# A two-layer hybrid encoder in one kernel: a fixed issue order around the early gates, and the second layer's modulation computed in the first layer

## The chip, the cores and the metric

The kernel runs on one core of a Trainium2 chip. The metric is the device time of one execution in microseconds, and the time before is the median of three runs. TensorE multiplies, VectorE, ScalarE and GpSimd work element by element, SyncE (SP) only issues DMAs; ScalarE issues some DMAs too. Each engine takes its own instructions in a fixed order, and engines wait for one another through semaphores.

## The reference

The input is x (1024 tokens, 1024 channels, f32) and a vector c. Each of two layers does:

```
mod = silu(c) @ w_mod[l] + b_mod[l]           # sh1, sc1, g1, sh2, sc2, g2: six parts of 1024
h = rms_norm(x) * (1 + sc1) + sh1
y = mixer(h) @ w_out[l]                       # four head groups A, B, C, D over w_in[l]
x = x + g1 * rms_norm(y)
h = rms_norm(x) * (1 + sc2) + sh2
u = dwconv3(h @ w_up[l])                      # 2 x 2816 channels, 3 taps along the tokens
y = (gelu(u_gate) * u_value) @ w_down[l]
x = x + g2 * rms_norm(y)
```

The mixer is windowed attention (A), a short gated convolution (B), latent attention (C) and dilated windowed attention in three patterns (D).

## The kernel before

Channels lie on the partitions, tokens on the free axis; x and y are eight tiles of 128 x 1024. f32 operands are split into a high and a low fp32r half (`split`, L110 and L111: ScalarE copies the high half, GpSimd or VectorE subtracts for the low one), and a product is three matmuls, high x high, high x low and low x high.

A tile framework orders the work. The program is traced in Python; each engine's order is fixed ahead of the run by a list scheduler that, with a cost model, takes the ready instruction that was traced first. A helper `issue_after(ins)` adds an edge: every instruction traced in its block on the engine of `ins` is queued behind `ins`. Waits on data are added by the framework. Buffers are named by pool and tag, and a new tile of a tag waits until the older one in its place is free.

One layer goes through these stages:

- `mixer` (layer 0 up to 765 us, layer 1 from about 1700 to 2380). `group_d` computes values, keys and queries of the three patterns of D; between them it traces the modulation vectors of its own layer (`modulations`, parts 2, 4 and 3). One modulation part is 16 pieces: a 256 KB load of w_mod on SP and one VectorE instruction that accumulates (L360, L362), then a fold (L416 to L439).
- `project_out`, in two halves of 512 tokens. After each half comes `token_half`: `residual` (root of the mean square by `rstd`: squares on ScalarE at L164, column totals on TensorE at L158 with some added up on VectorE or GpSimd at L171, the root on VectorE from L176; then the scaling and x, L513 and L514), and `dense_input`, which does a second `rstd`, scales (L471), shifts (L474) and splits into `hh`, `hl`. For the second half `dense_input` goes through four pairs of tiles and also builds the sums that a Strassen-like product needs: t1 to t4, split into halves like the rest.
- `dense_up`: 22 pairs of a gate tile and a value tile, each by seven products of quarters (12 matmuls each) in place of eight. For the first six pairs (`ahead`) the two quarters that need only the first half's tokens run early, as `begin`: 12 matmuls into a bank `pj`, a copy to the tile u (L1238), 12 more into the same bank, a second copy (L1242), then the tile is stored to `kept`. Their weights (`early`) are loaded ahead of the second `token_half`, but the products are traced behind it. Then the weight sums of each pair (`sums`: two 512 KB loads, L1257 to L1262 on VectorE, three splits), the products of the first two pairs tile by tile (L1333), the four others of `ahead` (`kept_pair`), the rest, and after each pair `gated`: the convolution (first tap L934 on ScalarE for the gate of the first eight pairs, L936 on VectorE for all others; L938), GELU, the product (L1308) and a store.
- `dense_down`: blocks of two to four rows of tiles (`whole`, eight output tiles each; L1409 copies, L1411 adds to y), the rest in token halves (`some`, L1418), then the end of the layer. Layer 0 also does three modulation parts here ((0,5), (1,1) and (1,0)): `advance(2)` traces two pieces behind each output tile's addition, through two buffers `mr`. What is left over is traced before the end of the layer, which needs the room of these buffers.

`early`, `begin` and `sums` take their weight tiles in turn from three pairs of one pool and two of another (`pair`).

Of the kernel before, what the change touches and what calls it, by code (L numbers as in the profile page):

```python
# [9 lines left out]
F32 = mybir.dt.float32  # L10
F32R = mybir.dt.float32r
# [8 lines left out]
D = 1024  # L20
# [72 lines left out]
class Trunk:  # L93
# [51 lines left out]

    def rstd(self, tiles, n, temp, adders=None):

# [314 lines left out]

    def dense_input(self, y, l, half, temp, adders):

        nc, hs = self.nc, HALVES[half]
        rs = self.rstd([t[:, hs] for t in y], D, temp, adders)

        def normal(k):  # L470
            nc.vector.scalar_tensor_tensor(y[k][:, hs], y[k][:, hs], self.col(l, 2, k), rs, op0=ALU.mult, op1=ALU.mult)  # L471

        def shifted(k):
            nc.scalar.activation(y[k][:, hs], y[k][:, hs], AF.Identity, bias=self.shift(l, 3, k))  # L474

        if half == 0:
            for k in (0, 4, 1, 5, 2, 6, 3, 7):
                normal(k)
                shifted(k)
                self.split(self.hh[k][:, hs], self.hl[k][:, hs], y[k][:, hs], nc.gpsimd if k % 2 else nc.vector)  # L480
            return
        n1, n2 = HALVES
        self.t2, self.t3, self.t4w = [], [], []
        for i in range(4):
            j = 4 + i
            a, b, t12 = y[i], y[j], temp("x")
            t1, t2, t3, t4 = t12[:, n1], t12[:, n2], temp("sq"), temp("t")
            normal(i)
            normal(j)
            shifted(j)  # L490
            nc.vector.scalar_tensor_tensor(t1, a[:, n2], self.shift(l, 3, i), a[:, n1], op0=ALU.add, op1=ALU.subtract)
            nc.vector.tensor_sub(t2, b[:, n2], t1)
            nc.vector.tensor_sub(t4, b[:, n1], t2)
            nc.vector.tensor_sub(t3, t2, a[:, n1])
            self.split(self.hh[i][:, n2], self.hl[i][:, n2], t1, nc.vector)
            self.split(self.hh[j][:, n2], self.hl[j][:, n2], b[:, n2], nc.gpsimd if i % 2 else nc.vector)
            for to, k, t, eng in ((self.t2, i, t2, None), (self.t4w, None, t4, nc.vector), (self.t3, j, t3, None)):
                room = self.te.tile([128, 1024], F32R, name="t4", tag=f"t4{i}") if k is None else self.new_y(k, F32R)
                self.split(room[:, n1], room[:, n2], t, eng)
                to.append((room[:, n1], room[:, n2]))  # L500

# [595 lines left out]
    def mixer(self, l):  # L1097
        tc, nc = self.tc, self.nc
        with ExitStack() as e:
# [4 lines left out]
            with ExitStack() as e2:  # L1104
# [90 lines left out]
    def quarter(self, ps, w, at, xs, first=True, last=True, order=None):  # L1195
# [6 lines left out]
        for i, (xh, _) in enumerate(xs):  # L1202
            ks = slice(at + 128 * i, at + 128 * i + 128)
            nc.tensor.matmul(ps, w[1][:, ks], xh, start=False, stop=last and i == len(xs) - 1, skip_group_check=True)  # L1204

    def dense_up(self, l, early):
# [5 lines left out]
        n1, n2 = HALVES  # L1212
        b11 = [(self.hh[i][:, n1], self.hl[i][:, n1]) for i in range(4)]
        b21 = [(self.hh[i][:, n1], self.hl[i][:, n1]) for i in range(4, 8)]
# [3 lines left out]
        c1, c2 = slice(1, 513), slice(513, 1025)  # L1218
        ahead = 6
        kept = self.kept  # L1220
        with tc.tile_pool(name=f"ux{l}", bufs=2, reuse_waits="tile") as ux, \
# [4 lines left out]
            def u_tile():  # L1226
# [5 lines left out]
                return u  # L1232

            def begin(u, w1, between=None):

                x = self.pj.tile([128, 512], F32, name="pj", tag="pj")
                self.quarter(x, w1, 0, b11)
                nc.scalar.activation(u[:, c2], x, AF.Copy)  # L1238
                if between:
                    between()  # L1240
                self.quarter(x, w1, 512, b21, False)
                nc.scalar.activation(u[:, c1], x, AF.Copy)  # L1242

            def sums(t, whole):

                gate, sums = self.pair(F32)
                nc.sync.dma_start(gate, self.a["w_up"][l, t])
                raw = self.raw.tile([128, 1024], F32, name="raw", tag="raw")
                nc.sync.dma_start(raw, self.a["w_up"][l, FT + t])
                a11, a12, a21, a22 = (r[:, h] for r in (gate, raw) for h in HALVES)  # L1250
                w1 = self.pair() if whole else None
                w2, w3 = self.pair(), self.pair()
                if whole:
                    self.split(*w1, gate)
                w4 = [a2p.tile([128, 512], F32R, name=t, tag=t) for t in ("vh", "vl")]
                s1, s2 = sums[:, 0:512], sums[:, 512:1024]
                nc.vector.tensor_add(s1, a21, a22)  # L1257
                nc.vector.tensor_sub(s2, s1, a11)
                self.split(*w4, a22)

                nc.vector.tensor_sub(a21, a11, a21)
                nc.vector.tensor_sub(a22, a12, s2)  # L1262
                self.split(*w2, sums)
                self.split(*w3, raw)
                return w1, w2, w3, w4

# [35 lines left out]
            def gated(t, us):  # L1302
                cv = [self.tmp(x) for x in "ab"]
                for o, u, m in zip(cv, us, (t, FT + t)):
                    base = _P["fconv"] + l * 132 + m
                    self.conv3(o, u, lambda i: self.par[:, base + 44 * i:base + 44 * i + 1], m == t < ahead + 2)
# [5 lines left out]
            for t in range(ahead):  # L1312
                u = u_tile()
                begin(u, early[t] if t < len(early) else self.up_weight(l, t))
                nc.scalar.dma_start(kept[128 * t:128 * t + 128, :], u[:, 1:1025])

            def kept_pair(t):
                ws, u = sums(t, False), u_tile()
                nc.sync.dma_start(u[:, 1:1025], kept[128 * t:128 * t + 128, :])
                return Pair(u, ws)  # L1320


            two = [kept_pair(t) for t in range(2)]
            jobs = []
# [15 lines left out]
            for t in range(2, FT):  # L1340
                if t < ahead:
                    p = kept_pair(t)
                    p.head()
                else:
                    ws, u = sums(t, True), u_tile()
                    p = Pair(u, ws)
                    begin(u, ws[0], p.head)
                gated(t, p.tail())

    def dense_down(self, l, y, end):  # L1350
# [3 lines left out]
        with tc.tile_pool(name=f"dq{l}", bufs=4, reuse_waits="tile") as dq:  # L1354
# [96 lines left out]
    def run(self):  # L1451
# [13 lines left out]
        self.vd = [dram.tile([S, 260], F32, name=f"vd{p}") for p in range(2)]  # L1465
        self.brep = [dram.tile([4, 128, n], F32, name=f"brep{i}") for i, n in enumerate(OH_LEN)]
        self.setup()
        xsrc = a["x"]
# [30 lines left out]
        for l in range(DEPTH):  # L1499
# [108 lines left out]
```

## Time and profile before

| what | value |
|---|---|
| median of 3 runs | 3244.16 us (3235.51 to 3247.09) |
| profiled execution | 3242.23 us, span 3240.4 us |
| TensorE (PE) busy | 2884.5 us, 89%, 13178 matmuls |
| VectorE (DVE) busy | 2385.1 us, 74% |
| ScalarE (ACT) busy | 1159.5 us, 36% |
| GpSimd (POOL) busy | 1157.2 us, 36% |
| mean granted TensorE clock | 0.952 of full speed |
| DMA | 305.32 MB, 94 GB/s over the span |

All times inside the run count from the start of the span. A matmul of 128 x 128 by 128 x 512 is listed with about 0.4 us since matmuls overlap in the pipeline; how closely they follow each other is seen from their count in a stretch. "x6" behind a line is the number of merged instructions, and the brackets behind it give the idle time of the engine before the first of them and what ended it.

### The profile page before, as it was taken

The numbers are of one execution on the slowest core, as the hardware profiler recorded it, in microseconds if no ns is written. First come the engines' busy times: TensorE is split into PE (matmuls) and PEld (weight loads), VectorE is DVE, ScalarE is ACT, GpSimd is POOL, SyncE is SP. The second block draws the span as 40 slices with busy tenths as digits, with TensorE's granted clock in tenths as the row PEclk, the third lists the DMA queues.
The fourth block names the chain that finished last, engine by engine and source line by source line (L and its number), as shares of the span: only waits on it lengthen the run. The fifth ranks groups of instructions, "written<-read, shape, count | busy, mean of one in ns | idle before, by whom it ended". The sixth has DMA issues, their size and how long they took to land. (4 is left out here: it accounts for less than half of the span.)

```text
span 3240.4 us, 35414 instructions
## 1 busy us (share of the span) xinstructions
PE 2884.5 (89%) x13178; PEld 2291.8 (71%) x13178; DVE 2385.1 (74%) x3196; ACT 1159.5 (36%) x1674; POOL 1157.2 (36%) x821
## 2 busy tenths in 40 slices
PE   7888989988959999999979889898887789999997
PEld 3677767776637778878756777677765668887886
DVE  6687567697558888867767875577965798886556
ACT  4231443554433333331243223435534433234121
POOL 1221133324344554542532212232244545455231
PEclk8998999999979999999989999999998999999999
DMA  5225111102333222254422341110123232224323
GB/s 201 80 91 183 55 37 34 56 20 78 104 110 110 84 80 78 85 195 162 156 94 62 120 149 50 40 47 27 46 73 129 101 114 85 85 78 141 133 91 104
DMA packets 122680, 305.32 MB, mean 94 GB/s; under 512 B 13403, under 2 KB 32091, under 8 KB 122508
## 3 DMA queue, kind: packets, MB, share of 16 engines
q1 hardware_dynamic: 113868, 284.19, 26.6%
q10 hardware_dynamic: 8640, 18.88, 1.5%
q8 instruction: 103, 1.69, 0.2%
q14 instruction: 69, 0.57, 0.1%
HBM read 244.38 MB, written 62.03 MB: 95 GB/s over the span
## 5 line engine op out<-in xcount | busy, mean ns | idle before, releaser
L111 POOL TENSOR_TENSOR wl<-raw,wh 128x1024 fp32r<-128x1024 f32 (+2 forms) x82 | 203.8, 2486 | 468.4 <-ACT wh L110 259.0
L530 PE MATMUL pj<-hh,wh 128*128 128x512 f32 x800 | 331.1, 414 | 25.5 <-DVE ks L561 14.7
L531 PE MATMUL pj<-hl,wh 128*128 128x512 f32 x800 | 325.7, 407 | 6.4 <-POOL hl L459 5.3
L534 PE MATMUL pj<-hh,wl 128*128 128x512 f32 x800 | 210.7, 402 | 0.0
L530 PEld LDWEIGHTS pj<-hh,wh 128*128 128x128 f32 x800 | 156.6, 196 | 68.2 <-issue 30.6
L531 PEld LDWEIGHTS pj<-hl,wh 128*128 128x128 f32 x800 | 156.2, 195 | 44.1 <-POOL hl L459 7.3
L534 PEld LDWEIGHTS pj<-hh,wl 128*128 128x128 f32 x800 | 153.5, 193 | 36.3 <-issue 1.0
L690 PE MATMUL po<-s,v 128*96 128x128 f32 (+3 forms) x672 | 133.4, 360 | 43.8 <-ACT s L687 43.7
L690 PE MATMUL po<-hp,v 128*96 128x256 f32 x512 | 126.4, 402 | 36.3 <-ACT hp L687 35.9
L690 PEld LDWEIGHTS po<-s,v 128*96 128x96 f32 x672 | 99.3, 187 | 72.7 <-ACT s L687 56.2
L111 POOL TENSOR_TENSOR ul<-raw,uh 128x1024 fp32r<-128x1024 f32 x45 | 120.6, 2680 | 70.2 <-ACT uh L110 70.1
L577 ACT ACTIVATE qh<-pj 64x512 fp32r<-64x512 f32 x128 | 107.2, 837 | 99.4 <-PE pj L534 51.5
L110 ACT ACTIVATE wh<-raw 128x1024 fp32r<-128x1024 f32 (+2 forms) x90 | 94.0, 1044 | 134.4 <-PE pj L531 76.9
L938 DVE SCALAR_TENSOR_TENSOR ta<-u,par,ta 128x1024 f32<-128x1024 f32 x88 | 138.9, 1578 | 1.4 <-ACT ta L934 1.4
L1411 DVE TENSOR_TENSOR y<-y,po 128x1024 f32<-128x1024 f32 x60 | 73.0, 1218 | 90.4 <-PE po L523 90.4
L690 PEld LDWEIGHTS po<-hp,v 128*96 128x96 f32 x512 | 85.8, 172 | 71.4 <-ACT hp L687 44.0
L579 DVE TENSOR_TENSOR ql<-pj,qh 64x512 fp32r<-64x512 f32 x64 | 55.5, 867 | 107.3 <-ACT qh L577 106.5
L938 DVE SCALAR_TENSOR_TENSOR tb<-u,par,tb 128x1024 f32<-128x1024 f32 x88 | 128.2, 1457 | 0.0
L111 POOL TENSOR_TENSOR pl<-raw,ph 128x1024 fp32r<-128x1024 f32 x26 | 66.2, 2551 | 168.2 <-ACT ph L110 108.0
L677 PE MATMUL psc<-qh,ks 128*128 128x256 f32 (+2 forms) x272 | 88.3, 339 | 38.9 <-DVE s L805 15.2
L560 ACT ACTIVATE ks<-pj 64x512 fp32r<-64x512 f32 x56 | 49.0, 876 | 163.8 <-PE pj L534 96.5
L561 DVE TENSOR_TENSOR ks<-pj,ks 64x512 fp32r<-64x512 f32 x56 | 51.0, 911 | 73.6 <-ACT ks L560 72.8
(613 smaller groups left out, 8988.2 us busy)
## 6 DMA issues: line engine op xcount, KB each, us to landing
raw<-in_w_up_dram SPq DMA_DIRECT2D x56, 512.0 KB, 3.6
raw<-in_w_in_dram SPq DMA_DIRECT2D x52, 512.0 KB, 3.3
raw<-in_w_down_dram SPq DMA_DIRECT2D x50, 512.0 KB, 3.7
mr<-in_w_mod_dram SPq DMA_DIRECT2D x96, 256.0 KB, 3.0
room<-in_w_mod_dram SPq DMA_DIRECT2D x96, 256.0 KB, 3.4
actd<-ta SPq DMA_DIRECT2D x44, 512.0 KB, 2.6
uh<-in_w_up_dram SPq DMA_DIRECT2D x26, 512.0 KB, 3.7
xd<-y ACTq DMA_DIRECT2D x48, 256.0 KB, 3.6
```

The source lines that it names most:

```text
L110: self.nc.scalar.activation(hi, src, AF.Copy)
L111: (eng or self.nc.gpsimd).tensor_sub(lo, src, hi.bitcast(F32))
L530: nc.tensor.matmul(ps, wh[:, ks], self.hh[k][:, hs], start=k == 0, stop=False, skip_group_check=True)
L531: nc.tensor.matmul(ps, wh[:, ks], self.hl[k][:, hs], start=False, stop=False, skip_group_check=True)
L534: nc.tensor.matmul(ps, wl[:, ks], self.hh[k][:, hs], start=False, stop=k == KT - 1, skip_group_check=True)
L561: nc.vector.tensor_sub(lo, src, hi.bitcast(F32))
L577: nc.scalar.activation(self.perm(qh[h][o:o + 64], r)[:, n * half:n * half + n, :], src, AF.Copy)
L579: nc.vector.tensor_sub(lo, src, own.bitcast(F32))
L677: nc.tensor.matmul(ps, ks[:, c], qh[:, q0:q1], start=first, stop=False, skip_group_check=True)
L690: nc.tensor.matmul(o[0:96, co], v(tt, h), s[:, cs], start=co.start // 512 not in seen, stop=False, skip_group_check=True)
L938: nc.vector.scalar_tensor_tensor(o, t[:, i:i + n], cw(i), o, op0=ALU.mult, op1=ALU.add)
L1411: self.mark = nc.vector.tensor_add(d, d, p)
```

## The change

- In the second half's `token_half` the order of tracing becomes: residual, the six early gates (`begin_early`), the weight sums of the first two pairs, and only then `dense_input`. The early gates alternate between two tiles of u (they had four) and skip the memsets of the edge columns; the first two pairs' w4 halves lie in tiles `ta` and `tb`.
- Edges in `dense_input` of the second half: the first four squares behind gate 1's second copy, the last four behind gate 2's (both on ScalarE), the totals behind gate 3's last matmul (on TensorE), and what ScalarE does for the four pairs of tiles behind the second copies of gates 4, 5, 5 and 5.
- The modulation parts 2, 4 and 3 of layer 1 leave the second mixer. The list of pieces in layer 0 has six parts in place of three; the up-projection of layer 0 traces one piece after each of the pairs 6 to 21, and the large blocks of `dense_down` three behind each output tile in place of two.
- The first tap of the convolution is on ScalarE for the gate of all 22 pairs.

```diff
 rstd:
-            nc.scalar.activation(sq, t, AF.Square)
+            with self.queued(after and after[0][i]):
+                nc.scalar.activation(sq, t, AF.Square)
             if eng is nc.tensor:
-                total(sq, first, i == len(tiles) - 1 and not accs)
+                with self.queued(after and after[1]):
+                    total(sq, first, i == len(tiles) - 1 and not accs)
 dense_input:
+        rs = self.rstd([t[:, hs] for t in y], D, temp, adders,
+                       after and ([after[1][1]] * 4 + [after[2][1]] * 4, after[3][0]))
...
         for i in range(4):
+            with self.queued(after[min(4 + i, len(after) - 1)][1]):
...
+    def queued(self, ins):
+        return self.tc.issue_after(ins.ins) if ins is not None else ExitStack()
 mixer:
-                self.group_d(l, self.modulations(l))
+                self.group_d(l, self.modulations(l) if l == 0 else iter(()))
+    def begin_early(self, l, ws):
+        nc, done = self.nc, []
+        for t in range(self.ahead):
+            u = self.t4.tile([128, 1026], F32, name="u", tag=("tc", "tn")[t % 2])
+            done.append(self.begin(u, ws[t] if t < len(ws) else self.up_weight(l, t)))
+            nc.scalar.dma_start(self.kept[128 * t:128 * t + 128, :], u[:, 1:1025])
+        return done
 dense_up:
-                    self.conv3(o, u, ..., m == t < ahead + 2)
+                    self.conv3(o, u, ..., m == t)
-            two = [kept_pair(t) for t in range(2)]
+            two = [kept_pair(t, ws) for t, ws in enumerate(early)]
...
                 gated(t, p.tail())
+                if t >= ahead:
+                    self.advance(1)
 dense_down, whole:
-                        self.advance(1 if len(ops) < 4 else 2)
+                        self.advance(1 if len(ops) < 4 else 3)
 run:
-                self.pieces = self.modulate([(0, 5), (1, 1), (1, 0)] if l == 0 else [])
+                self.pieces = self.modulate([(0, 5), (1, 1), (1, 0), (1, 2), (1, 4), (1, 3)] if l == 0 else [])
...
-                        for part in token_half(1, self.temps(bd, x="few")):
-                            part()
+                        t = self.temps(bd, x="few")
+                        token_half(1, t)[0]()
+                        done = self.begin_early(l, early)
+                        early = [self.sums(l, k, False, self.t4) for k in range(2)]
+                        self.dense_input(y, l, 1, t, adders[1], done)
```

`begin`, `sums` and `quarter` become methods with the same body; `begin` returns its last matmul and its last copy.

## Rows read from the trace of the kernel before

**Rows 1.** Stretches: length, PE, PEld, DVE, ACT, POOL busy us, PEclk, DMA share, GB/s
```profile
1085.00:1370.00 285.00, 283.52 (x1226) 230.64 (x1225) 240.88 (x232) 93.84 (x119) 143.31 (x116) 1.00 0.24 84
1370.00:1570.00 200.00, 196.70 (x857) 160.42 (x856) 141.26 (x149) 56.02 (x62) 89.59 (x36) 1.00 0.53 176
...
1830.00:1860.00 30.00, 23.50 (x97) 18.67 (x96) 28.75 (x38) 9.11 (x13) 9.57 (x4) 0.89 0.65 211
1860.00:1890.00 30.00, 26.99 (x209) 26.59 (x210) 22.56 (x50) 4.36 (x10) 0.53 (x5) 0.94 0.70 213
1890.00:1930.00 40.00, 31.56 (x140) 25.06 (x138) 30.39 (x38) 17.27 (x18) 10.11 (x7) 0.91 0.42 139
1930.00:1985.00 55.00, 50.42 (x312) 44.30 (x312) 18.55 (x21) 18.64 (x22) 7.82 (x9) 1.00 0.22 73
```

**Rows 2.** Waits of PE, 840 to 1000: us in total, times, longest
```profile
PE pj L1200 <- ACT u L1238: 29.6, 1, 29.6
PE po L158 <- ACT sq L164: 7.5, 3, 4.6
```

**Rows 3.** Timeline of ACT, layer 0: start, us, engine, line, operation
```profile
875.34 0.60 ACT L1165 ACTIVATE y<-pw 128x512 f32<-128x512 f32 x1 [6.57 <-PE pw L523]
...
917.62 0.72 ACT L474 ACTIVATE y<-y,mod 128x512 f32<-128x512 f32 x1 [2.97 <-DMA kept<-u]
...
946.73 0.58 ACT L1238 ACTIVATE u<-pj 128x512 f32<-128x512 f32 x1
```

**Rows 4.** Waits of PE, 2474 to 2580 (layer 1)
```profile
PE pj L1200 <- ACT u L1238: 9.9, 2, 8.1
PE po L158 <- ACT sq L164: 9.6, 3, 8.2
```

**Rows 5.** Timeline of DVE, layer 0
```profile
911.96 0.72 DVE L176 STREAM_TRANSPOSE t<-po 128x512 f32<-128x512 f32 x1 [10.23 <-PE po L158]
...
918.17 0.75 DVE L471 SCALAR_TENSOR_TENSOR y<-y,gm,acc 128x512 f32<-128x512 f32 x1
...
922.44 1.75 DVE L471 SCALAR_TENSOR_TENSOR y<-y,gm,acc 128x512 f32<-128x512 f32 x1
...
946.17 0.68 DVE L111 TENSOR_TENSOR t<-t,t 128x512 fp32r<-128x512 f32 x1
```

**Rows 6.** Timeline of POOL, layer 0
```profile
901.08 1.77 POOL L514 TENSOR_TENSOR y<-y,x 128x512 f32<-128x512 f32 x1 [1.97 <-DMA x<-in_x_dram]
...
947.94 1.28 POOL L111 TENSOR_TENSOR y<-sq,y 128x512 fp32r<-128x512 f32 x1
...
953.65 2.41 POOL L111 TENSOR_TENSOR ul<-ul,uh 128x1024 fp32r<-128x1024 f32 x1 [1.90 <-ACT uh L110]
```

**Rows 7.** Timeline of PE: last product of the first two pairs, both layers
```profile
990.70 0.39 PE L1333 MATMUL pj<-y,ul 128*128 128x512 f32 x1
...
2575.28 0.39 PE L1333 MATMUL pj<-y,ul 128*128 128x512 f32 x1
```

**Rows 8.** Timeline of DVE, layer 1
```profile
2510.01 0.72 DVE L176 STREAM_TRANSPOSE t<-po 128x512 f32<-128x512 f32 x1 [11.48 <-PE po L158]
...
2546.45 0.68 DVE L111 TENSOR_TENSOR t<-t,t 128x512 fp32r<-128x512 f32 x1
```

**Rows 9.** Stretches of the tile room (modulation), sum over 1700 to 1985
```profile
sum 285.00, DVE 51.41; mean DVE 7.34
```

**Rows 10.** Timeline of SP, layer 0's down-projection
```profile
1425.73 23.97 SPq L357 DMA_DIRECT2D mr<-in_w_mod_dram x12
```

**Rows 11.** The tile mr: ns min/median/max, first and last start, and landing of its DMAs
```profile
L362 DVE SCALAR_TENSOR_TENSOR mc<-mr,cact,mc x56: 736/751/2775, 1417.8 to 3046.9; 128x512 f32<-128x512 f32 x56
...
DMA to landing us min/median/max: 2.7/3.0/5.4
```

**Rows 12.** Timeline of DVE, layer 0's down-projection
```profile
1482.04 1.21 DVE L1411 TENSOR_TENSOR y<-y,po 128x1024 f32<-128x1024 f32 x1
```

**Rows 13.** Line 934: who waited for it, us, times
```profile
PEld psc L1200: 6.2, 2
```

More of the change, by code (lines that the diff above doesn't have):

```diff
@@ L144, in spread, with rstd @@
                                  r.unsqueeze(2).broadcast_to([n, f, 32]))
-    def rstd(self, tiles, n, temp, adders=None):
+    def rstd(self, tiles, n, temp, adders=None, after=None):
         nc = self.nc
@@ L461, in modulated, with dense_input @@
                 nc.vector.scalar_tensor_tensor(hl, t, sh, hh.bitcast(F32), op0=ALU.add, op1=ALU.subtract)
-    def dense_input(self, y, l, half, temp, adders):
+    def dense_input(self, y, l, half, temp, adders, after=None):
         nc, hs = self.nc, HALVES[half]
-        rs = self.rstd([t[:, hs] for t in y], D, temp, adders)
+        rs = self.rstd([t[:, hs] for t in y], D, temp, adders,
+                       after and ([after[1][1]] * 4 + [after[2][1]] * 4, after[3][0]))
         def normal(k):
@@ L484, in dense_input @@
         for i in range(4):
[L485 to L500, printed above, removed]
+            with self.queued(after[min(4 + i, len(after) - 1)][1]):
+                j = 4 + i
+                a, b, t12 = y[i], y[j], temp("x")
+                t1, t2, t3, t4 = t12[:, n1], t12[:, n2], temp("sq"), temp("t")
+                normal(i)
+                normal(j)
+                shifted(j)
+                nc.vector.scalar_tensor_tensor(t1, a[:, n2], self.shift(l, 3, i), a[:, n1], op0=ALU.add, op1=ALU.subtract)
+                nc.vector.tensor_sub(t2, b[:, n2], t1)
+                nc.vector.tensor_sub(t4, b[:, n1], t2)
+                nc.vector.tensor_sub(t3, t2, a[:, n1])
+                self.split(self.hh[i][:, n2], self.hl[i][:, n2], t1, nc.vector)
+                self.split(self.hh[j][:, n2], self.hl[j][:, n2], b[:, n2], nc.gpsimd if i % 2 else nc.vector)
+                for to, k, t, eng in ((self.t2, i, t2, None), (self.t4w, None, t4, nc.vector), (self.t3, j, t3, None)):
+                    room = self.te.tile([128, 1024], F32R, name="t4", tag=f"t4{i}") if k is None else self.new_y(k, F32R)
+                    self.split(room[:, n1], room[:, n2], t, eng)
+                    to.append((room[:, n1], room[:, n2]))
     def residual(self, y, l, g, hs, xsrc, dst, temp, adders=None, rs=None):
@@ L1203, in quarter, with begin, sums @@
             ks = slice(at + 128 * i, at + 128 * i + 128)
-            nc.tensor.matmul(ps, w[1][:, ks], xh, start=False, stop=last and i == len(xs) - 1, skip_group_check=True)
+            mm = nc.tensor.matmul(ps, w[1][:, ks], xh, start=False, stop=last and i == len(xs) - 1, skip_group_check=True)
+        return mm
+    def begin(self, u, w1, between=None):
+        nc = self.nc
+        b11, b21 = ([(self.hh[i][:, HALVES[0]], self.hl[i][:, HALVES[0]]) for i in range(k, k + 4)] for k in (0, 4))
+        x = self.pj.tile([128, 512], F32, name="pj", tag="pj")
+        self.quarter(x, w1, 0, b11)
+        nc.scalar.activation(u[:, 513:1025], x, AF.Copy)
+        if between:
+            between()
+        product = self.quarter(x, w1, 512, b21, False)
+        return product, nc.scalar.activation(u[:, 1:513], x, AF.Copy)
+    def begin_early(self, l, ws):
[5 more added lines that the diff above has]
+        return done
+    def sums(self, l, t, whole, pool):
+        nc = self.nc
+        gate, sums = self.pair(F32)
+        nc.sync.dma_start(gate, self.a["w_up"][l, t])
+        raw = self.raw.tile([128, 1024], F32, name="raw", tag="raw")
+        nc.sync.dma_start(raw, self.a["w_up"][l, FT + t])
+        a11, a12, a21, a22 = (r[:, h] for r in (gate, raw) for h in HALVES)
+        w1 = self.pair() if whole else None
+        w2, w3 = self.pair(), self.pair()
+        if whole:
+            self.split(*w1, gate)
+        if pool is self.t4:
+            room = pool.tile([128, 1026], F32R, name="v", tag=("ta", "tb")[t])
+            w4 = room[:, 0:512], room[:, 512:1024]
+        else:
+            w4 = [pool.tile([128, 512], F32R, name=t, tag=t) for t in ("vh", "vl")]
+        s1, s2 = sums[:, 0:512], sums[:, 512:1024]
+        nc.vector.tensor_add(s1, a21, a22)
+        nc.vector.tensor_sub(s2, s1, a11)
+        self.split(*w4, a22)
+        nc.vector.tensor_sub(a21, a11, a21)
+        nc.vector.tensor_sub(a22, a12, s2)
+        self.split(*w2, sums)
+        self.split(*w3, raw)
+        return w1, w2, w3, w4
     def dense_up(self, l, early):
@@ L1217, in dense_up @@
         t2, t3, t4 = self.t2, self.t3, self.t4w
-        c1, c2 = slice(1, 513), slice(513, 1025)
-        ahead = 6
-        kept = self.kept
+        c1, c2, ahead = slice(1, 513), slice(513, 1025), self.ahead
         with tc.tile_pool(name=f"ux{l}", bufs=2, reuse_waits="tile") as ux, \
@@ L1232, in u_tile @@
                 return u
[L1234 to L1265, printed above, removed]
             class Pair:
@@ L1309, in gated, with kept_pair @@
                 nc.sync.dma_start(self.actd[128 * t:128 * t + 128, :], cv[0])
[L1312 to L1319, printed above, removed]
+            def kept_pair(t, ws=None):
+                ws, u = ws or self.sums(l, t, False, a2p), u_tile()
+                nc.sync.dma_start(u[:, 1:1025], self.kept[128 * t:128 * t + 128, :])
                 return Pair(u, ws)
-            two = [kept_pair(t) for t in range(2)]
+            two = [kept_pair(t, ws) for t, ws in enumerate(early)]
             jobs = []
@@ L1466, in run @@
         self.brep = [dram.tile([4, 128, n], F32, name=f"brep{i}") for i, n in enumerate(OH_LEN)]
+        self.ahead = 6
         self.setup()
```

8 lines of the change are left out of this document (3 added, 5 removed).

## The prediction

> **What bounds the kernel now.** I read the table by stretches first: it tells which stage has idle TensorE time at all. In the steady part of the first up-projection TensorE is busy 283.52 of 285 us with 1226 products, 0.2325 us each, and in the first down-projection 196.70 of 200; there only what delays TensorE counts, and VectorE (240.88 of 285 us) is cover [rows 1]. Three places have idle TensorE time and are touched by the change. The waits of TensorE name the first: in layer 0 one wait of 29.6 us, on ScalarE's copy at L1238 [rows 2]. ScalarE's own order shows why: before that copy, at 946.73, stands all that begins with L474 at 917.62, the second half's shifts and high halves, which come at VectorE's pace [rows 3]. The early gates are free for TensorE, their product is ready, but its bank is emptied 29 us late. In layer 1 the same wait is 9.9 us in two pieces, since the order there happened to put copies between the splits [rows 4]. The third place is the second mixer at 1830 to 1930, where VectorE is busy 81.70 of 100 us and TensorE 82.05 [rows 1], and the modulation, from 1812 to 1920, is 51.41 us of vector time [rows 9].
>
> **The change part by part.** The sum is made against the profiled execution, 3242.23 us (span 3240.4); the median of the three runs is 3244.16, 1.9 higher, and is added at the end.
>
> *Early gates ahead of the second half's input, layer 0.* Six gates issue 24 products each (5.6 us), two copies on ScalarE and one store on ScalarE's queue; nothing of it is new, and 24 memsets of one column go from GpSimd, off any chain: nothing. What ends this stage is a chain: last residual row ready (902.85, GpSimd L514), squares, totals, reciprocal root (VectorE starts at 911.96), the split of eight tiles on VectorE until 946.85, the last low half on GpSimd until 949.22, then the products of the first two pairs until 991.09 [rows 5, 6, 7].
> New waits: the squares 0 to 3 queue on ScalarE behind gate 1's second copy, 4 to 7 behind gate 2's, the totals on TensorE behind gate 3's last product. Behind the waiting squares stand the next copies, and TensorE waits for these. The totals now have two more gates ahead, 48 products or 11.2 us; the room for it is the 7.5 us that TensorE now waits for the squares [rows 2]. So the root starts 3.7 us later, 915.7. The splits' waits, behind the copies of gates 4 and 5, cost nothing: those products follow the totals directly and take 11.2 us, while the root and the first four vector steps take some 7; if the cover were short, 4 us.
> The weight sums of the first two pairs move ahead of the splits, with everything they issue: four 512 KB loads on SP (behind the residual's x loads, which are issued first), eight vector adds of 0.6 us, six high halves on ScalarE, six low halves on GpSimd, four of 2.41 us [rows 6] and two of half a tile. The first pair's fall into VectorE's idle time before the root; of the second pair's four adds (2.4 us) three of the first pair's stand in the stretch already (1.8): +0.6. The low halves compete with VectorE: the same step takes 0.75 us alone and 1.75 beside a GpSimd low half [rows 5]. For the second pair's three I put 4 us, between 0 (they fall elsewhere) and 12.2 (all six, whole).
> So the splits end at 915.7 + 34.9 + 0.6 + 4 = 955.2, the last low half 2.4 later. Most products of the two pairs, which go tile by tile, now run beside the splits; left are the last tile's 21 and one quarter of 12, 33 x 0.2325 = 7.7 us: 965.3. In the kernel before the same point is 991.09 less the 8 products (1.9 us) that were done ahead of it: 989.2. Gain 24 us, between 10 and 32.
>
> *The same, layer 1.* The root starts at 2510.01 and the splits end at 2547.13 [rows 8]; the totals' room is 9.6 us [rows 4], so +1.6. One low half of the sums lies in that stretch already, so +2 for GpSimd and +0.6: 2511.6 + 37.1 + 2.6 = 2551.3, then 2.4 and 7.7: 2561.4, against 2575.67 - 1.9 = 2573.8 [rows 7]. Gain 12, between 0 and 20.
>
> *No modulation in the second mixer.* 48 loads of 256 KB, 48 accumulations and three folds leave 1812 to 1920. From 1830 to 1930 TensorE is busy 23.50, 26.99 and 31.56 us at granted clocks 0.89, 0.94 and 0.91 of 2.4 GHz; at full clock that is 75.0 us of work. The stretch after it, 1930 to 1985, without modulation, has 50.42 busy of 55 at clock 1.00, a share of 0.917 [rows 1]. At that share the work takes 81.8 of the 100 us: gain 18. Ends: 25 (no idle time is left) and 0 (the gaps are latencies of the evictions, not of VectorE's queue). What is late next is TensorE.
>
> *Where it goes.* The pieces come into layer 0: 16 into the up-projection, one per pair, and 35 more into the down-projection with its tail, 3 per output tile where there were 2. In the up-projection 16 x 0.75 us [rows 11] go onto VectorE, whose first taps of the gate (28 in the kernel) go to ScalarE at the same time; TensorE covers both, 0 us; without cover 12 us. The taps on ScalarE wait for the store of the tile before, and TensorE waited for such a tap 6.2 us over the 16 there are [rows 13]; for 28 more that is 10.9 at most, in pairs with far more slack; I take 1.
> In the down-projection the two buffers set the pace: 12 loads in a row took 23.97 us on SP [rows 10], 2.15 us per piece (23.64 over 11 intervals), 6.45 us for three, against 24 x 0.2325 = 5.58 us of TensorE per output tile. That is 0.87 x 21 = 18 us late; the accumulator banks let TensorE run two tiles ahead (11.2 us), so 7 us come through, between 0 and 35 (no banks ahead, and the 16 left over at 2.15 us = 34 us beside two passes of 96 products, 44.6). Layer 1 has 17 pieces as before: nothing.
>
> Sum: 24 + 12 + 18 - 1 - 7 = 46 us. 3242.2 - 46 = 3196.2, on the scale of the median 3198.
>
> **A rule against it.** VectorE's step beside a GpSimd low half grows by 1.0 us [rows 5]; a low half of that size takes 1.28 alone [rows 6]. The Trainium skill (SBUF — State Buffer, Who interferes with whom) says that a VectorE instruction with two SBUF inputs and a GpSimd instruction that reads SBUF exclude each other for the whole instruction. By that rule what stands above as 4 and 2 us would be up to the low halves' whole time; the next rival works this out from rows.
>
> **The rivals.**
> (a) GpSimd blocks the chain. If all six low halves of a layer fall between root and last split and each stops VectorE for its length, 4 x 2.41 + 2 x 1.3 = 12.2 us come in, instead of 4 and 2 (layer 1 has one of them already: 12.2 - 2.4 = 9.8): 16 us more, 3214. For: L471 at 1.75. Against: VectorE idles ten microseconds ahead of the root, and the first pair's are ready then.
> (b) The totals are queued behind all six gates: they are traced later. Then the root comes 11.2 us later still in each layer: 3198 + 22 = 3220. For: six gates are ready at that point. Against: gate 5's weight comes late, from a buffer that gate 0 frees.
> (c) The order does nothing: in layer 1 two thirds of the wait had gone by themselves, and in layer 0 the wait would turn up at the weights (GpSimd's low halves) or at the splits. Then 18 - 8 = 10 are left: 3232.2, 3234 as a median. For: VectorE's 35 us of splits stay on the chain. Against: the wait of 29.6 us has three gates of ready work behind it, 72 products.
> (d) Slower. Place: the three large blocks of layer 0's down-projection. VectorE takes its queue in order; if each of three pieces waits for its load and the eviction (1.21 us) [rows 12] stands behind them, a tile costs 3p + 1.21 against 5.58. From p = 2.49 us on this eats the other gains (54 + 11.2 us over 21 tiles = 3.1 each). With the longest landing seen, 5.4 us [rows 11], and 0.75 of use, two buffers give p = 3.08: 4.87 x 21 - 11.2 = 91 us, 3242.2 - 54 + 91 = 3279, 3281 as a median. For: p is 2.15 already and weights share the SP queue. Against: the median landing is 3.0.
>
> **How the numbers follow.** Forecast 0.53 (its own range 3180 to 3212), (a) 0.10, (b) 0.15, (c) 0.13, (d) 0.09. What a measurement of this kernel can tell from no change is about 0.5%, 16 us: 3228 to 3260. The forecast, (a) and (b) are faster, 0.78; (c) is within, 0.13; (d) is slower, 0.09. The predicted time is the forecast's, 3198. The range 3165 to 3238 holds the first four and both ends of the mixer's gain; it reaches down to every term at its best (32 + 20 + 25 = 77 us: 3167) and leaves out (d).
>
> **What will show it.** Right: no wait on L1238 over 3 us beside the splits in layer 0, and the last product of the two pairs some 90 us after the copy of the last output tile (875.94 [rows 3], so 115 now) and in layer 1 too; the root at most 5 us later than now; second mixer's stretch from first to last key projection 15 to 20 us shorter, VectorE without L362 there; in layer 0's down-projection TensorE idle under 10 us more. Wrong: totals behind gate 5's products, VectorE steps of 1.75 us and more throughout the splits, or weight loads queued on SP behind pieces with TensorE waiting for `wl` or for L1411.

## The result, and the profile after

The changed kernel is slower: 3268.51 us median of 4 runs (3265.27 to 3276.93) against 3242.34 (3235.51 to 3247.09) of the kernel before on the same chip, a ratio of 1.0086 [1.0059, 1.0114]. The forecast was 3198. The profiled execution after took 3276.93 us, the longest of its four; its last product ends 34 us later than in the trace of before.

Each layer is cut at the same points in every trace: the last product of the output projection, of the first two pairs, the gate product of pair 7, the last product of the up-projection, the totals at the layer's end, the first product of the next output projection. Lengths in us, worked out from the timelines:

| stretch | before | after | change | predicted |
|---|---|---|---|---|
| up to the end of layer 0's output projection | 875.3 | 877.5 | +2 | 0 |
| early gates and first pairs, layer 0 | 115.8 | 93.6 | -22 | -24 |
| to the gate product of pair 7 | 132.2 | 135.0 | +3 | 0 |
| pairs 8 to 21, layer 0 | 258.5 | 268.5 | +10 | +1 with the taps |
| down-projection, layer 0 | 243.5 | 287.8 | +44 | +7 |
| end of layer 0 and second mixer | 717.6 | 695.9 | -22 | -18 |
| output projection, layer 1 | 130.4 | 132.9 | +2 | 0 |
| early gates and first pairs, layer 1 | 102.4 | 101.7 | -1 | -12 |
| to the gate product of pair 7 | 131.4 | 133.8 | +2 | 0 |
| pairs 8 to 21, layer 1 | 257.5 | 261.1 | +4 | 0 |
| down-projection and end, layer 1 | 259.7 | 270.9 | +11 | 0 |

No edit touches the first stretch, yet it took 874.5 to 884.5 us in the traces of all kernels here; the whole time of a single trace carries this spread.

Stretches of the changed kernel, with the columns of [rows 1]: first pairs 8 to 21 of layer 0, then most of its down-projection, then the part of the second mixer that held the modulation.

```profile
1106.10:1374.60 268.50, 260.03 (x1117) 208.62 (x1116) 220.06 (x209) 96.71 (x122) 133.39 (x102) 1.00 0.29 95
...
1374.60:1450.00 75.40, 69.39 (x289) 55.55 (x287) 47.75 (x54) 27.10 (x29) 34.95 (x14) 0.95 0.54 183
1450.00:1503.00 53.00, 46.74 (x192) 37.72 (x192) 42.30 (x59) 9.21 (x9) 18.08 (x7) 0.93 0.57 184
1503.00:1560.00 57.00, 48.84 (x204) 39.37 (x204) 38.85 (x53) 7.84 (x10) 12.24 (x6) 0.95 0.54 173
...
1868.00:1898.00 30.00, 29.86 (x168) 25.53 (x167) 12.82 (x25) 11.07 (x17) 7.26 (x4) 1.00 0.28 89
1898.00:1921.00 23.00, 23.00 (x167) 21.73 (x167) 0.00 (x0) 4.02 (x8) 3.07 (x8) 1.00 0.38 117
```

The mixer did what it should: in place of 0.89 to 0.94 the granted clock is 1.00, and the products that lay between 1830 and 1930 now take about 79 us. The down-projection, which ran at 196.70 busy of 200 [rows 1], now has TensorE idle and a clock of 0.93 to 0.95. The waits of TensorE in it (after, 1374.6 to 1658.4) say on whom:

```profile
PE po L525 <- DVE y L1428: 18.6, 5, 6.5
PE pd L525 <- DVE y L1435: 7.2, 4, 2.5
PE po L525 <- ACT y L1426: 2.8, 1, 2.8
```

L1428 and L1435 are the additions that empty the banks (before: L1411 and L1418). The same waits of before, 1381.8 to 1621.3, sum to 5.2 us:

```profile
PE pd L521 <- DVE y L1418: 2.0, 1, 2.0
PE po L522 <- DVE pl L111: 1.6, 1, 1.6
PE po L521 <- ACT y L1409: 1.6, 2, 1.3
```
VectorE's own order, in one place of the changed kernel, shows why the addition is late:

```profile
1486.68 0.75 DVE L364 SCALAR_TENSOR_TENSOR mc<-mr,cact,mc 128x512 f32<-128x512 f32 x1 [0.41 <-DMA mr<-in_w_mod_dram]
1488.60 0.75 DVE L364 SCALAR_TENSOR_TENSOR mc<-mr,cact,mc 128x512 f32<-128x512 f32 x1 [1.17 <-DMA mr<-in_w_mod_dram]
1490.45 0.75 DVE L364 SCALAR_TENSOR_TENSOR mc<-mr,cact,mc 128x512 f32<-128x512 f32 x1 [1.10 <-DMA mr<-in_w_mod_dram]
1491.12 1.22 DVE L1428 TENSOR_TENSOR y<-y,po 128x1024 f32<-128x1024 f32 x1
```

Each piece takes 0.75 us but stands in the queue until its load lands; the addition has to wait behind three of them. The tile mr of the changed kernel (as [rows 11]) sums these waits to 44.7 us over the whole kernel, where the view of before has 7.1, and SP's queue (as [rows 10]) shows the pace, (30.13 - 0.33) / 14 = 2.13 us per load:

```profile
L364 DVE SCALAR_TENSOR_TENSOR mc<-mr,cact,mc x98: 736/751/2892, 1106.0 to 3055.4; 128x512 f32<-128x512 f32 x98
...
  DVE mc L364: 44.7, 47
...
DMA to landing us min/median/max: 2.7/3.1/5.6
```
```profile
  DVE mc L362: 7.1, 11
```
```profile
1424.97 30.13 SPq L359 DMA_DIRECT2D mr<-in_w_mod_dram  x15
```

At the early gates, the answers to [rows 2] (after, 842 to 1002) and [rows 4] (2491 to 2593), and to the roots of [rows 5, 8] on VectorE:

```profile
PE po L1348 <- ACT hx L110: 6.6, 1, 6.6
...
PE pj L1208 <- ACT u L1221: 4.0, 2, 2.5
```
```profile
PE pj L1208 <- ACT u L1221: 10.0, 1, 10.0
PE po L1348 <- ACT hx L110: 6.6, 1, 6.6
```
```profile
932.72 0.72 DVE L178 STREAM_TRANSPOSE t<-po 128x512 f32<-128x512 f32 x1 [8.23 <-PE po L158]
...
2554.49 0.72 DVE L178 STREAM_TRANSPOSE t<-po 128x512 f32<-128x512 f32 x1 [9.76 <-PE po L158]
```

The 29.6 us wait of layer 0 is gone. But the root starts 55 us after the output projection's last product, where it was 37; in layer 1 63, where it was 37. A new wait of 10 us stands in layer 1. ScalarE's order ahead of it:

```profile
2505.90 0.60 ACT L1225 ACTIVATE u<-pj 128x512 f32<-128x512 f32 x1 [1.59 <-POOL y L518]
2509.40 4.99 ACTq L519 DMA_DIRECT2D xd<-y  x4
2514.49 0.40 ACTq L1233 DMA_DIRECT2D kept<-u  x1
2518.06 0.81 ACTq L519 DMA_DIRECT2D xd<-y  x2
2518.92 1.09 ACT L1221 ACTIVATE u<-pj 128x512 f32<-128x512 f32 x2 [12.42 <-DMA kept<-u]
```

L519 stores the residual's rows from ScalarE's queue. Each store stands there until its row is done, and the next gate's copy (L1221) behind it. The bracket names another wait, for the landing of the store of u: the early gates now alternate between two tiles of u where they had four. How much goes with the stores of the rows is tested below (stores_from_sync); no run gives the gates four tiles again.

### The profile page after: what moved, and what is told of

It reads as the page before. It is cut to its first block, busy times and chain, and to the rows that moved or that the text cites. A ratio compares the mean times of both kernels' runs of the same rounds, so it can differ in the third digit from the quotient of the medians.

```text
span 3275.2 us, 35394 instructions
## 1 busy us (share of the span) xinstructions
PE 2909.4 (89%) x13178; PEld 2299.8 (70%) x13178; DVE 2339.0 (71%) x3168; ACT 1185.3 (36%) x1702; POOL 1151.7 (35%) x797
## 5 line engine op out<-in xcount | busy, mean ns | idle before, releaser
L946 DVE SCALAR_TENSOR_TENSOR ta<-u,par,ta 128x1024 f32<-128x1024 f32 x88 | 154.9, 1761 | 34.2 <-ACT ta L942 34.1
L698 PE MATMUL po<-hp,v 128*96 128x256 f32 x512 | 126.5, 403 | 37.1 <-ACT hp L695 36.7
L698 PEld LDWEIGHTS po<-s,v 128*96 128x96 f32 x672 | 101.3, 190 | 71.6 <-ACT s L695 54.7
L946 DVE SCALAR_TENSOR_TENSOR tb<-u,par,tb 128x1024 f32<-128x1024 f32 x88 | 137.3, 1560 | 0.0
L364 DVE SCALAR_TENSOR_TENSOR mc<-mr,cact,mc 128x512 f32<-128x512 f32 x98 | 98.1, 1001 | 45.1 <-DMA mr<-in_w_mod_dram 44.7
L1428 DVE TENSOR_TENSOR y<-y,po 128x1024 f32<-128x1024 f32 x60 | 72.7, 1216 | 69.5 <-PE po L527 69.4
```

The costliest lines, as they stand in the source:

```text
L364: nc.vector.scalar_tensor_tensor(acc, w, s, acc, op0=ALU.mult, op1=ALU.add)
L698: nc.tensor.matmul(o[0:96, co], v(tt, h), s[:, cs], start=co.start // 512 not in seen, stop=False, skip_group_check=True)
L946: nc.vector.scalar_tensor_tensor(o, t[:, i:i + n], cw(i), o, op0=ALU.mult, op1=ALU.add)
L1428: self.mark = nc.vector.tensor_add(d, d, p)
```

## The experiments

Every kernel was timed against the kernel before. Ratios with their 95% intervals:

| run | what | median us | ratio to before |
|---|---|---|---|
| after | the change | 3268.51 | 1.0086 [1.0059, 1.0114] |
| order_alone | order only | 3223.03 | 0.9932 [0.9915, 0.9950] |
| move_alone | modulation's move only | 3269.88 | 1.0083 [1.0063, 1.0102] |
| pace_two | after, two pieces per tile | 3261.32 | 1.0048 [1.0030, 1.0065] |
| one_load_in_eight | after, most loads left out | 3224.02 | 0.9936 [0.9920, 0.9952] |
| third_buffer | after, three buffers | 3248.62 | 1.0021 [1.0009, 1.0034] |
| taps_back | after, taps on VectorE | 3254.01 | 1.0042 [1.0026, 1.0058] |
| move_two_per_pair | after, pieces spread | 3241.24 | 0.9998 [0.9988, 1.0009] |
| totals_behind_gate_one | order, bounds earlier | 3227.31 | 0.9954 [0.9940, 0.9967] |
| stores_from_sync | order, stores on SP | 3219.43 | 0.9935 [0.9918, 0.9952] |
| gates_behind_totals | that, gates 3 to 5 later | 3201.88 | 0.9878 [0.9861, 0.9896] |
| move_one_third | stores_from_sync, a third moved | 3215.77 | 0.9918 [0.9904, 0.9932] |
| both_of_these | the last two together | 3195.12 | 0.9855 [0.9838, 0.9872] |

### The two halves apart

```diff
 # order_alone: after, but
-self.group_d(l, self.modulations(l) if l == 0 else iter(()))
+self.group_d(l, self.modulations(l))
-    if t >= ahead: self.advance(1)          # dense_up
-self.advance(1 if len(ops) < 4 else 3)
+self.advance(1 if len(ops) < 4 else 2)
 # list of pieces: three parts; taps: m == t < ahead + 2
 # move_alone: before, with exactly these four lines the other way round, taps as before
```

> The issue order of squares, totals and splits and the first pairs' sums, in both layers; the modulation and the taps as in the kernel before. If the segments of the changed kernel add up: +22 us in layer 0 (last output tile to the end of the first pairs), -3 in its kept pairs, +1 in layer 1, -2 in its kept pairs, -2 in its output projection: some 16 us faster than before, 3226 on a median of 3242. If the gain of layer 0 in the changed kernel came from less work on VectorE elsewhere (taps on ScalarE): under 8 us. If the order's loss is what made the whole change slower: slower than before.

> The kernel before with the modulation of the second mixer moved to layer 0's up- and down-projection, nothing else. If the move is the loss: second mixer -25, pieces in the up-projection +6, down-projection of layer 0 +44, three pieces per tile in layer 1's +8: 33 us slower, 3275. If the down-projection was late for another reason (the new order or taps upstream): 25 faster to equal, 3217 to 3242.

The order alone is 22 us faster, by its ratio, the move alone 27 slower. By stretches the order gives 22.0 us in layer 0 and 1.1 in layer 1, and the pairs right behind lose 1 and 2. The move gives 25.6 in the mixer and loses 40.3 in layer 0's down-projection, 1 in the up-projection, 6.5 in layer 1's end. So the down-projection is late with the old order too. Together the halves are 5 us slower; the changed kernel with its taps put back (below) is 14, and the 9 between lie inside the intervals of the three. TensorE's waits there (move_alone, 1382.6 to 1662.5) are on the same addition:

```profile
PE po L521 <- DVE y L1413: 17.5, 4, 6.0
PE pd L521 <- DVE y L1420: 5.7, 4, 2.2
```

### What makes the pieces late

```diff
 # pace_two: after, but
-self.advance(1 if len(ops) < 4 else 3)
+self.advance(1 if len(ops) < 4 else 2)
 # one_load_in_eight: after, but in mod_pieces (layer 0's list and layer 1's end)
-    w = self.mr.tile([128, 512], F32, name="mr", tag="mr")
-    nc.sync.dma_start(w, ...)
+    if k == 0:
+        w = self.mr.tile([128, 512], F32, name="mr", tag="mr")
+        nc.sync.dma_start(w, ...)
 # third_buffer: after, but pieces of layer 0's down-projection take mx, mr, mr in turn
+self.mrs = cycle((<pool "mx", bufs=1>, self.mr, self.mr))
```

> The changed kernel with two pieces per output tile instead of three; 37 are left for the tail of layer 0's down-projection instead of 16. If three pieces per tile through two buffers are too fast for their loads: the blocks keep their old pace, layer 0's down-projection gets 35 to 44 us back and layer 1's 8: 3268 - 48 = 3220. If the loads are too slow at any place, the tail's 37 pieces at 2.1 us (78 us) compete with the evictions of its products and it gives back half: 3245. If VectorE's queue was not the cause: 3268, unchanged.

> The changed kernel, but of each eight loads of modulation weights only the first is issued and the other seven accumulations read the same tile again; the loads left out are 84 of 96 in layer 0, and what is computed for the modulation is not the reference's. VectorE's accumulations stay. If it is the wait for the loads that stands in VectorE's queue ahead of the evictions: TensorE's idle time in layer 0's down-projection falls from 36 to under 10 us and the kernel is 35 to 45 us faster than the changed one, 3228. If it is VectorE's own work (three pieces of 0.75 us and two evictions per tile): no gain, 3268.

> The changed kernel with a third buffer for the modulation's pieces in layer 0's down-projection (the 2 KB that are left there); three pieces per output tile as before. If the pace of 2.1 us per piece is two buffers against the landing of a load, it becomes 1.4 and three take 4.3 us, less than a tile's 5.58: 25 to 34 of the 44 us come back, 3268 - 30 = 3238. If the transfers themselves set the pace (DMA engines busy 0.56 to 0.68 there): the waits stay, 3260 to 3268.

I split the down-projection at the last addition of the large blocks (from the end of the up-projection; then the tail to the layer-end totals):

| kernel | blocks | tail |
|---|---|---|
| before | 186.5 | 57.0 |
| after | 216.5 | 71.3 |
| pace_two | 189.6 | 107.5 |
| one_load_in_eight | 190.9 | 62.7 |
| third_buffer | 201.3 | 65.5 |

Without the loads 34 of the 44 us are gone though VectorE still does all accumulations: the waits for the loads are the loss, its own work is the smaller part. The edit also takes traffic off the DMA queues, but what TensorE waited for in the changed kernel were the additions; on a weight of the blocks it waited 0.6 us. It also leaves out 14 of 16 loads at layer 1's end, which is 15 us shorter than in the changed kernel, so the 44.5 us of the whole kernel are not all layer 0's. With two pieces per tile the blocks are whole again; TensorE's waits of pace_two from 1379.4 to 1580 are the eviction at the start (the blocks are 3.1 us longer than before) and little else:

```profile
PE po L525 <- ACT y L1426: 2.8, 1, 2.8
PE po L526 <- DVE wl L111: 0.6, 1, 0.6
PE po L525 <- DVE u L1320: 0.5, 1, 0.5
```

But I had expected 3220 and it is 3261: the pieces left over are all traced ahead of the layer's end, and what had been lost in the blocks is lost in the tail, most of it in one wait for the statistics of the first half, for the next layer (pace_two, 1580 to 1680). They need that half's residual, and its root stands on VectorE among pieces that wait: it takes the totals at 1621.00, and its next step runs at 1650.78.

```profile
PE po L158 <- DVE ta L173: 32.6, 1, 32.6
```
```profile
1621.00 0.72 DVE L178 STREAM_TRANSPOSE tn<-po 128x512 f32<-128x512 f32 x1 [0.57 <-PE po L158]
...
1650.78 0.17 DVE L180 TENSOR_SCALAR sm<-tn 128x16 f32<-128x16 f32 x1
```

The down-projection with the stretch behind it is 3 us shorter than in the changed kernel; most of pace_two's gain is layer 1's end, 12.8 us shorter.

With a third buffer SP issues 17 loads in 27.60 us, (27.60 - 0.33) / 16 = 1.70 us each, where two buffers gave 2.13:

```profile
1429.81 27.60 SPq L359 DMA_DIRECT2D mr<-in_w_mod_dram  x17
```

So the buffers set the pace and not the transfers alone (two thirds of 2.13 would be 1.42, so they are not all of it). The kernel is 0.65% faster than the changed one by the ratios, some 21 us, and that is the 21.0 us that its down-projection is shorter; I had expected 25 to 34 of the 44.

### The taps

```diff
 # taps_back: after, but
-    self.conv3(o, u, ..., m == t)
+    self.conv3(o, u, ..., m == t < ahead + 2)
```

> The changed kernel with the gate's first taps of pairs 8 to 21 back on VectorE, in both layers. If the taps on ScalarE are what pairs 8 to 21 lost (9.9 us in layer 0, 3.6 in layer 1; with pieces but with taps on VectorE they lost 1): 13 us faster than the changed kernel, 3255. If the 9.9 us of layer 0 are the pieces' load on VectorE, the taps on VectorE add 28 x 0.6 us there: 3268 or slower.

As the first theory had it. Pairs 8 to 21 take 260.8 us in layer 0, where the changed kernel takes 268.5; of the 10.0 us lost there 7.7 are the taps and 2.3 the pieces. VectorE waited 34.1 us in the changed kernel for a tap on ScalarE (who waited for L942); before, in the view of [rows 13], it was 1.4 us:

```profile
  DVE ta L946: 34.1, 18
```
```profile
  DVE ta L938: 1.4, 1
```

### Where pieces have room

```diff
 # move_two_per_pair: after with the taps back, but
-    if t >= ahead: self.advance(1)
+    self.advance(2)                          # every pair from 2 on
-self.advance(1 if len(ops) < 4 else 3)
+self.advance(2)
 # move_one_third: stores_from_sync (below), but the list gets (1, 2) alone, modulations(1)
 # keeps parts 4 and 3, dense_up advance(1) from pair 6, dense_down 2 as before
```

> The changed kernel with the taps back on VectorE and the pieces spread otherwise: two for each of the 20 pairs from 2 on in layer 0's up-projection (40), two per output tile in the down-projection (56), 6 left for its tail. If three pieces per tile and the leftover in the tail were the loss: the order's 19 and the mixer's 25 us stay, less 3 to 8 for VectorE in the up-projection: 3242 - 38 = 3204. If the pieces cost 0.75 us of VectorE each wherever they are: 40 x 0.75 = 30 us come back in the up-projection, 3230. If two loads wait there as in the blocks, slower than 3240.

> The order alone with the stores on SyncE's queue, and one of the three modulations of the second mixer moved: one piece for each of pairs 6 to 21 in layer 0's up-projection, two per output tile in the down-projection as before, so nothing more in the blocks than before and 3 left for the tail. If free places for pieces exist only at about one per pair: the mixer gains a third of 25, the up-projection loses 1 to 2: 3219 - 7 = 3212. If each moved piece costs what it brings: 3219.

Two per pair was a miss: 3241. The mixer's gain came (23.2 us), but pairs 8 to 21 lost 14.6, against 1.3 with one per pair in move_alone, and the down-projection 18. VectorE has no room for a second piece (move_two_per_pair, 1200 to 1300; before it was 85.74 busy in the same 100 us and TensorE 100.00):

```profile
1200.00:1300.00 100.00, 97.81 (x422) 78.88 (x421) 97.70 (x92) 31.39 (x41) 52.74 (x41) 1.00 0.32 106
```

Why the down-projection lost 18 at the old pace isn't settled: some 10 pieces ran in its tail, and VectorE came late out of the up-projection. With one third moved, the mixer is 8.6 us shorter, the up- and down-projection 1.7 and 1.6 longer. That leaves 5 us, which the times alone don't separate from stores_from_sync (the intervals overlap).

### Why the root came late

```diff
 # totals_behind_gate_one: order_alone, but
-([after[1][1]] * 4 + [after[2][1]] * 4, after[3][0])
+([after[0][1]] * 4 + [after[1][1]] * 4, after[1][0])
 # stores_from_sync: order_alone, but
-(nc.sync if dst is self.a["out"] else nc.scalar).dma_start(dst..., yk)
+(nc.sync if dst is self.a["out"] or (g == 1 and hs.start) else nc.scalar).dma_start(dst..., yk)
 # gates_behind_totals: stores_from_sync with the bounds of totals_behind_gate_one, and
-done = self.begin_early(l, early)             # gates 0 to 5, then the sums
+done = self.begin_early(l, early, range(3))
+# inside dense_input, after its rstd: gates 3 to 5 queued on TensorE behind the last total,
+# then the sums; the splits behind the copies of gates 3, 4, 5, 5
```

> The order alone, with each bound two gates earlier: squares 0 to 3 behind gate 0's copy, 4 to 7 behind gate 1's, the totals behind gate 1's product instead of gate 3's. If the root waits for the totals that stand behind the gates on TensorE (it comes 36 us after the last residual row in layer 1 and VectorE is idle before it): the root comes 10 to 20 us earlier and the pairs end 8 to 15 us earlier in each layer, 3223 - 22 = 3201. If TensorE's own work sets the stretch (gates, totals and pairs are the same number of products): no gain, 3223.

> The order alone, with the eight stores of the second half's residual rows issued from SyncE's queue instead of ScalarE's, in both layers. If ScalarE's gate copies wait behind stores that wait for their rows: the 9.5 us wait of TensorE in layer 1 on a copy (2474 to 2483) falls under 3, and 5 to 8 us come out in layer 1: 3217. If the stores then stand in front of SyncE's weight loads: the wait turns up at the weights, no gain: 3223.

> The order alone with the stores on SyncE's queue, and gates 3 to 5 held on TensorE behind the totals (squares behind gates 0 and 1, totals behind gate 1, splits behind gates 3 to 5, the pairs' sums traced behind the gates). If the totals' place behind the gates is what makes the root late (36 us after the last residual row in layer 1, 28 in layer 0): the root comes 10 to 15 us earlier in each layer and the pairs end 8 to 15 earlier: 3219 - 22 = 3197. If the chain behind the root (splits, sums now after it) grows by the same: 3219. If TensorE idles at the totals and the gates come late: slower than 3225.

> The two kernels before it together. If both gains hold they add up, 3197 - 7 = 3190; if neither, 3219.

With the bounds two gates earlier nothing moved: the totals of layer 0 still run from 921.50 to 932.7 on TensorE in totals_behind_gate_one, some 44 us after the output projection, as with the bound at gate 3.

```profile
921.50 1.88 PE L158 MATMUL po<-sq,ones 128*128 128x512 f32 x4
925.99 1.02 PE L158 MATMUL po<-sq,ones 128*128 128x512 f32 x2
928.88 2.97 PE L158 MATMUL po<-sq,ones 128*128 128x512 f32 x6 [1.87 <-ACT sq L165]
931.69 1.02 PE L158 MATMUL po<-acc,ones 128*128 128x512 f32 x2
```

An edge "behind gate 1" is a lower bound only. The gates are traced ahead of the squares, and the scheduler takes first what was traced first; that this is why the totals stay where they are fits, but the other way round is what shows it: with gates 3 to 5 held behind the totals the root starts 34.6 us after the output projection in layer 0 and 37.0 in layer 1 (gates_behind_totals):

```profile
917.98 0.72 DVE L178 STREAM_TRANSPOSE t<-po 128x512 f32<-128x512 f32 x1 [0.40 <-PE po L158]
...
2486.84 0.72 DVE L178 STREAM_TRANSPOSE t<-po 128x512 f32<-128x512 f32 x1 [5.24 <-PE po L158]
```

The root gains 21 us in layer 0 against order_alone, the stretch only 8.6 (93.8 to 85.2). A part of the rest stands on VectorE: from root to last split it now takes 42 us where the changed kernel takes 33.7. GpSimd's four long low halves of the weight sums now fall between root and last split; one of them takes 4.58 us, and behind it a split's own low half 4.00:

```profile
941.06 4.58 POOL L111 TENSOR_TENSOR ul<-wl,uh 128x1024 fp32r<-128x1024 f32 x1 [3.68 <-ACT uh L110]
...
955.38 4.00 POOL L111 TENSOR_TENSOR y<-x,y 128x512 fp32r<-128x512 f32 x1 [3.63 <-ACT y L110]
```

In layer 1 the same stretch is 86.5 us, where order_alone has 101.3. Of these 14.8 us 6.7 came with the stores on SP: there TensorE waits 2.1 us for the copy L1221 and not 9.5, but 3.8 for L1225 in place of 0.6. In the whole time stores_from_sync can't be told from order_alone. The two versions together reach 3195 us, 1.45% under the kernel before, the best of all runs; against gates_behind_totals alone the gain of the moved third is 7 us by the medians, and the intervals just overlap.

## Why the prediction was wrong

**The failed step: the down-projection, and in it the lead of two tiles.** It put +7 and measured +44. The pace was right: 2.15 us predicted, 2.13 measured. Three paces (6.45 us) also come near to what a tile cost: from the first to the last addition of a large block (L1428) VectorE took 47.0, 49.0 and 45.7 us, 6.5 to 7.0 for each of seven tiles, where it took 38.1 to 38.7 before. That is some 27 us over 21 tiles, and the prediction had 18. What failed is what I took off it, the 11.2 us that TensorE can run ahead. Inside a block it does run ahead: its tiles keep 5.4 to 5.5 us, and the additions fall back to as much as 12.7 us behind their products. But at the end of each block TensorE has to wait for them, and gives the lead back (after, L525 on TensorE):

```profile
1452.62 0.77 PE L525 MATMUL po<-qh 128*128 128x512 f32 x1 [4.72 <-DVE y L1428]
...
1505.03 0.76 PE L525 MATMUL po<-ph 128*128 128x512 f32 x1 [5.67 <-DVE y L1428]
...
1562.10 0.79 PE L525 MATMUL po<-wh 128*128 128x512 f32 x1 [6.51 <-DVE y L1428]
```

So the blocks lost 30.0 us where 7 were forecast. The tail lost 14.3 more for 14 pieces that the sum put at nothing: the prediction has the 16 left over only in the upper end, and doesn't show how 18 and 34 make its 35.

Rival (d) had the place. Its formula at the measured pace makes 3 x 2.13 + 1.21 = 7.6 us per tile and (7.6 - 5.58) x 21 - 11.2 = 31 us, which meets the 30.0 by luck: the tile took 6.5 to 7.0, and the lead wasn't kept. With two pieces per tile two paces and the addition are 5.47, under 5.58, and in pace_two the large blocks take 38.1 to 38.6 us as before. With a third buffer three paces are 5.1, under a tile's 5.58, and the formula gives 4 us; the blocks there lost 14.8, so neither the three paces nor the formula is the whole mechanism, and what else holds those tiles up stays open.

The waits of TensorE that are listed in the down-projection grew from 5.2 to 31.7 us; the other 18 of the 44 are longer busy time. The sum left out the clock. From the granted clock of the stretches (0.89 to 0.98 after, 0.97 to 1.00 before) I estimate some 13 of the 18 for it at most; the rest stays open. The runs don't show the clock as a loss of its own: without the loads TensorE waits 3.9 us in the blocks, and they are 4.4 us longer than before.

**Layer 0's early gates: right in size, not in the way.** 22 for 24. The root was to come 3.7 us later and came 18.5 later, as rival (b) had it: the totals run behind nearly all gates. This was made good elsewhere. The splits take 33.7 us, and no long low half of GpSimd falls among them, so rival (a) didn't happen in this form; and the last product is 4.7 us behind the last split where I had put 10.1. The splits were to take 39.5. So the root's 14.8 us too many were nearly made up by 5.8 and 5.4 too few behind it, and that 22 is near 24 is luck.

**Layer 1's early gates: wrong.** 0.7 for 12. The root came 63.3 us after the output projection in place of 36.7, 27 later where I had put 1.6: by the copy behind the stores on ScalarE's queue and by the totals: with the stores on SP it came at 56.3, with the later gates behind the totals as well at 37.0. I had counted the copies and the totals, but not the residual's eight stores that stand in that queue and wait for their rows.

**The taps and the up-projection: -1 and 0 against 7.7 + 2.3 in layer 0 and 3.6 in layer 1.** The bound of 10.9 was nearer than the value. The tap is no cover for the pieces: it brings its own wait to VectorE (34.1 us).

**The second mixer: 22 for 18,** inside the bounds of 0 and 25. TensorE was indeed next.

**Layer 1's end: 0 against 11.** It has 17 pieces as before, but they too run three per tile now; pace_two takes all 11 back.

**The forecast as a whole.** Of the rivals, (b) was true in its mechanism and (d) in its place, with half its price. "Order does nothing" (c) is excluded by order_alone at 0.9932, though in layer 1 the order by itself gave 1.1 us.

## What to carry to other kernels

Work that waits for a load costs the queue it stands in its whole wait, not its own time: price n pieces at n times the pace of their buffers and compare that with the time per tile. Don't take off what the engine behind can run ahead: here each block gave it back at its end. Count the pieces that are left over, too. An order edge "behind X" doesn't bring an instruction forward; to make the chain that sets the end run early, hold the other work behind it.

## What the runs showed of the hardware

- 256 KB loads used one after another came at 2.13 us each through two buffers (15 in a row), through three at 1.70 (17 in a row), with a landing of 3.1 us (median) in the changed kernel.
- A wait costs TensorE more than its length. With waits of 4.7 to 6.5 us in the down-projection the granted clock was 0.93 to 0.95 in the mean, where it had been 1.00 [rows 1], so a part of each stretch ran at 1.2 and not at 2.4 GHz. Behind the 9.5 us wait of order_alone (to 2483.4) 13 products took 5.30 us at a granted clock of 0.50, some 0.4 each; from 2488.7 on they follow each other by 0.23.

```profile
2483.40:2488.70 5.30, 5.29 (x13) 4.13 (x14) 0.00 (x0) 0.96 (x2) 1.27 (x1) 0.50 0.27 67
2488.70:2495.00 6.30, 6.30 (x28) 5.17 (x27) 2.59 (x4) 3.58 (x6) 1.51 (x1) 0.97 0.66 193
```

- Among VectorE's splits, GpSimd subtractions of 128 x 1024 took 4.58 us and one of 128 x 512 4.00, where 2.40 and 1.28 stand in the same trace (gates_behind_totals); VectorE's step of 0.75 us took up to 2.89 us in the changed kernel, beside a GpSimd subtraction of 128 x 1024. The Trainium skill (SBUF — State Buffer, Who interferes with whom) has such a pair exclude each other for the whole instruction; the trace agrees in kind, but no run isolated it.
